# Eight lasting weight buffers from the output projection into the FFN, and a new order of the first FFN chunks

## The chip, the cores and the metric

The kernel runs on one core of one Trainium2 chip. The metric is the device time of one execution in microseconds (us), as the median of several runs. Engines are called PE (TensorE), ACT (ScalarE), DVE (VectorE), POOL (GpSimd) and SP (SyncE, which issues the DMAs here).

## The reference: what is computed

One decoder layer on 1024 tokens of width 1024, all in float32. Its second part is what the change touches:

```
mix = concat(o_mla, o_dil) @ w_o                 # (1024,1024) @ (1024,1024)
x   = x + g1 * mix
h2  = rms_norm(x) * (1 + scale2) + shift2
u   = causal depthwise conv3(h2 @ w_up)          # w_up (1024, 5632), columns [gate | value]
x   = x + g2 * ((silu(gate) * value) @ w_down)   # w_down (2816, 1024)
```

Ahead of it stand the adaptive norm, the input projection, a dense attention and a dilated attention, each with 8 heads. Their output lies in an SBUF buffer `mix` (features on the partitions, 8 blocks of 128 by 1024 tokens).

## The kernel before, in words

Each float32 matrix product is made of three products of rounded parts: an operand is split into a high part (ACT copies it into a rounding type) and a low part (original minus high part, on POOL for weights and on DVE for most activations), and PE computes high·high, high·low and low·high (`mm3`, L102 to L105).

The instructions are traced in program order. A planner then fixes the order on each engine: it takes, at each point of its own estimate of time, the instruction traced earliest among those that are ready and whose tile has a free buffer. The engines run their lists strictly in order. A tile with a tag shares that tag's buffers; a new tile waits until the old one in its buffer has been used for the last time. Pools that are closed give their memory to pools opened later, tile by tile. `tc.issue_after(ins)` orders what is traced in the block behind `ins` on the engine of `ins`.

**Output projection** (L783 to L817). Two halves `hf` of four row blocks (128 tokens each); per half four column chunks `cch` of 256. A chunk loads 1 MB of `w_o` as raw [128, 8, 256], multiplies it by the gate row `g1row` on DVE (L795), and splits it (`split_weights`, L85 to L100: one ACT copy of 2048 columns, four POOL subtractions of 512). There are two sets of raw, high and low buffers, one in the pool `wstream2`, one in `wmore2`; both are closed after the projection (L820, L821). PE runs, for each of the four row blocks, seven feature blocks (k = 0 to 6), then for each the eighth, which is kept apart (`last_pair`: `lhi`, `llo`, one buffer each). DVE adds the residual (L810), ACT squares it for the norm; after the last chunk of a half `normalized` (L743 to L757) computes the reciprocal root and writes the normalized rows back into `mix`. `h2_half(0)` (transposes on PE, evacuation with gain and shift, split) runs within the second half of the projection.

**FFN, up** (L823 to L1009). `w_up` is taken in 22 chunks of 256 columns (`todo`: gate and value columns in turn). A raw chunk is [128, 8, 256], tag `raw`, two buffers; split weight pieces are [128, 2, 4, 128], tag `wa`, eight buffers, all in the pool `fp`, opened after the projection's pools are closed. From the third chunk on (n = 2) a chunk is computed by Strassen's scheme on 2x2 blocks: seven products (`step`, in the order 1, 2, 6, 5, 7, 3, 4) of weight combinations (`up_parts`: three pieces straight from raw, four by sums on DVE, L849, tag `sum`, four buffers) and activation combinations TB[1] to TB[7]. Each product is 12 matmuls of 512 columns (`block_mm`, L877). Chunks 0 and 1 are computed directly: `direct_mm` of 24 matmuls per 128 columns and half, the first half (`h2[., 0]`) before the second half's transposes `h2_half(1)` in the trace, the rest in `direct_rest`. Meanwhile DVE makes the differences b11 to b21 in place in `mix` (L974); two of them go through DRAM (`t_s`) and come back in `sum` buffers (L988), to be split into the T tiles of a pool that takes `mix`'s place (L983 to L989). Then the weights of chunk 2 are loaded and split (`ahead`, L996); each later chunk's weights are made during the chunk before.

**FFN, down** (L1012 on) uses the same tags `raw` and `wa`.

Of the kernel before, what the change touches and what calls it, by code (L numbers as in the profile page):

```python
# [8 lines left out]
F32 = mybir.dt.float32  # L9
# [4 lines left out]
ALU = mybir.AluOpType  # L14
# [27 lines left out]
def hybrid_layer(ctx, tc, x, c, positions, w_ada, b_ada, g_mix_norm, w_in, g_q_lat, w_q_b, g_kv_lat, w_kv_b,  # L42
# [570 lines left out]

    psum_phase(x=3, o=2, s=3)
    phM = ExitStack()
    mxp = phM.enter_context(tc.tile_pool(name="mixbuf", bufs=1, reuse_waits="tile"))
    mix = mxp.tile([P, 8, S], F32, name="mix")
    wst2 = ExitStack()
    wpool[0] = wst2.enter_context(tc.tile_pool(name="wstream2", bufs=1, reuse_waits="tile"))
    ap = phB.enter_context(tc.tile_pool(name="phB", bufs=1, reuse_waits="tile"))  # L620
# [94 lines left out]

    phE = ExitStack()
    wst3 = ExitStack()
    more_weight_buffers(wst3.enter_context(tc.tile_pool(name="wmore2", bufs=1, side="right", reuse_waits="tile")), 1)

    def slot(shape, dt, name, tag="mA"):  # L720
        return sp.tile(shape, dt, tag=tag, name=name, bufs=4 if tag == "x1" else 8)

    ep = phE.enter_context(tc.tile_pool(name="phE", bufs=1, reuse_waits="tile"))
# [58 lines left out]

    mixTs = [mix_tiles(t) for t in range(NT)]  # L783
    for hf in range(2):
        mixT = mixTs[4 * hf:4 * hf + 4]
        lp_ = last_pair(hf)
        x1 = [slot([P, D], F32, "x1", "x1") for _ in range(4)]
        sse = [ep.tile([P, 4], F32, tag="ssE", name="ssE", bufs=8) for _ in range(4)]
        for cch in range(4):
            cs = slice(cch * 256, cch * 256 + 256)  # L790
            raw = raw_tile(KD, 256)
            with tc.issue_after(first_load):
                nc.sync.dma_start(raw[:, 0:4, :], w_o[512:1024, cs].rearrange("(k p) n -> p k n", p=P))
                nc.sync.dma_start(raw[:, 4:8, :], w_o[0:512, cs].rearrange("(k p) n -> p k n", p=P))
            V.tensor_tensor(raw, raw, g1row[:, None, cs].to_broadcast([P, KD, 256]), op=ALU.mult)  # L795
            w = split_weights(raw, KD, 256)
            pss = []
            for i in range(4):
                ps = bank()
                for k in range(E7):  # L800
                    mm3(ps[:, 0:256], (mixT[i][0][:, k, :], mixT[i][1][:, k, :]), (w[0][:, k, :], w[1][:, k, :]),
                        k == 0, False)
                pss.append(ps)
            for i in range(4):
# [4 lines left out]
                mm3(pss[i][:, 0:256], (lp_[0][:, ts_], lp_[1][:, ts_]), (w[0][:, E7, :], w[1][:, E7, :]), False, True)  # L809
                V.tensor_tensor(x1[i][:, cs], pss[i][:, 0:256], xr, op=ALU.add)  # L810
                junk = ep.tile([P, 256], BF16, tag="junk", name="junkE", bufs=1)
                A.activation(junk, x1[i][:, cs], AF.Square, accum_out=sse[i][:, cch:cch + 1])
                if cch == 3:
                    nc.sync.dma_start(x1_s[t], x1[i])
                    normalized(hf, i, sse[i], x1[i])
            if hf == 1 and cch < 3:
                h2_half(0, ((0, 1, 2), (3, 4, 5), (6, 7))[cch])  # L817

    phE.close()
    wst3.close()  # L820
    wst2.close()  # L821
    psum_phase(X=2, Y=2, Z=2, x=2)
# [3 lines left out]
    for _ in range(4):  # L826
        fp.tile([P, S], F32, tag="y", name="y", bufs=4)
    def parts(src, hi, lo, eng):
        A.activation(hi, src, AF.Copy)  # L829
        eng.tensor_tensor(lo, src, hi.bitcast(F32), op=ALU.subtract)  # L830

    def up_raw(ff2, which):
        c0 = which * FF + ff2 * 256
        raw = fp.tile([P, KD, 256], F32, tag="raw", name="raw", bufs=2)
        nc.sync.dma_start(raw, w_up[:, c0:c0 + 256].rearrange("(k p) n -> p k n", p=P))
        return raw

    def up_parts(raw, direct=False):
        a11, a21 = raw[:, 0:4, 0:P], raw[:, 0:4, P:256]
        a12, a22 = raw[:, 4:8, 0:P], raw[:, 4:8, P:256]  # L840

        def put(n, src):
            wt = fp.tile([P, 2, 4, P], F32R, tag="wa", name="wa", bufs=8)
            parts(src, wt[:, 0, :, :], wt[:, 1, :, :], G)
            w[n] = wt
# [6 lines left out]
        w = {}  # L852
        if direct:
            for n, src in (((0, 0), a11), ((0, 1), a12), ((1, 0), a21), ((1, 1), a22)):
                put(n, src)
            return w
        put(1, a11)
# [15 lines left out]
    def block_mm(ps, wt, blocks, first):  # L873
        for kt in range(4):
            hi, lo = blocks[kt]
            for m, (a, b) in enumerate(((0, hi), (0, lo), (1, hi))):
                T.matmul(four(ps), lhsT=wt[:, a, kt, :], rhs=b, start=(first and kt == 0 and m == 0),  # L877
                         stop=(kt == 3 and m == 2), skip_group_check=True)

# [3 lines left out]
    def direct_mm(ps, w, u, hf):  # L883
        for half in range(2):
            blocks = [(four(h2[4 * half + kt, hf][:, 0, :]), four(h2[4 * half + kt, hf][:, 1, :])) for kt in range(4)]
            block_mm(ps, w[u, half], blocks, half == 0)

# [55 lines left out]

    todo = [(ff2, which) for ff2 in range(NFF // 2) for which in range(2)]
    w01 = [up_parts(up_raw(*a), True) for a in todo[0:2]]
    ps01 = [[bank(tag) for tag in "XY"] for _ in range(2)]
    for u in range(2):
        direct_mm(ps01[0][u], w01[0], u, 0)
    h2_half(1, range(KD))
    for u in range(2):  # L950
# [20 lines left out]
    for kt in range(4):  # L971
# [40 lines left out]
    def down_parts(ff):  # L1012
        if ff % 2 == 0:
            down_parts.raw = fp.tile([P, 2, D], F32, tag="raw", name="raw", bufs=2)
            nc.sync.dma_start(down_parts.raw, w_down[ff * P:(ff + 2) * P, :].rearrange("(u p) n -> p u n", p=P))
        raw = down_parts.raw[:, ff % 2, :]
        hi, lo = [fp.tile([P, D], F32R, tag="wa", name="wd", bufs=8) for _ in range(2)]
# [89 lines left out]
```

## Time and profile before

| | us |
|---|---|
| median of 3 runs | 1450.82 (1448.73 to 1451.15) |
| profiled execution, own time | 1452.97 |
| its span | 1451.0 |

| engine | busy us | share |
|---|---|---|
| PE | 1376.4 | 95% |
| DVE | 972.6 | 67% |
| POOL | 795.5 | 55% |
| ACT | 727.4 | 50% |

How to read it: times in the trace run from the span's start. PE's matmuls are pipelined, so the durations of neighbours overlap; the rate is seen from start to start or from a row with many of them. "Idle before, releaser" is how long an engine stood still before a row and what ended it. The granted clock (PEclk) is a share of full speed: at 0.5 PE runs at 1.2 GHz, at 1.0 at 2.4 GHz. The attention ends at about 649 us, the projection's products run from 652 to 751.7 us, the up part of the FFN follows and ends shortly before 1206 us, and the down part runs to the end.

### The profile page before, as it was taken

How to read it: one execution, taken by the hardware profiler on the slowest of the kernel's cores; microseconds unless marked ns; L12 is line 12 of the kernel's file. 1: busy time of each engine (PE TensorE's matmuls, PEld its weight loads, DVE VectorE, ACT ScalarE, POOL GpSimd, SP SyncE). 2: the span in 40 equal slices, each digit the busy share in tenths (PEclk: the TensorE clock that was granted, in tenths of full speed). 3: DMA queues.
4: the chain of work that ended last, by engine and by line, in shares of the span. 5: the costliest groups of instructions: out<-in, count | busy, mean ns of one | idle time of the engine just before them, and what ended most of it. 6: DMA issues, size and time to landing. Idle time of an engine off the chain costs nothing.

```text
span 1451.0 us, 22006 instructions
## 1 busy us (share of the span) xinstructions
PE 1376.4 (95%) x7837; PEld 1178.1 (81%) x7837; DVE 972.6 (67%) x1834; ACT 727.4 (50%) x1409; POOL 795.5 (55%) x780
## 2 busy tenths in 40 slices
PE   5889999998999998989989799999999999999998
PEld 3789999996778786779978688888888887888887
DVE  3667888687878888875655767777777765226213
ACT  3524322376778887864444644455455454322320
POOL 3355656367766667534624275656655554555552
PEclk9999999999999999999999899999999999999999
DMA  9643354546121114003535122222222238445431
GB/s 320 197 149 120 125 184 158 112 152 212 31 59 45 59 45 116 2 17 124 195 114 177 59 97 76 88 88 71 75 87 88 87 113 307 162 144 191 160 113 58
DMA packets 140197, 173.31 MB, mean 119 GB/s; under 512 B 7986, under 2 KB 118968, under 8 KB 139960
## 3 DMA queue, kind: packets, MB, share of 16 engines
q1 hardware_dynamic: 140088, 171.92, 36.5%
q8 instruction: 61, 1.00, 0.3%
q14 instruction: 48, 0.39, 0.1%
HBM read 135.19 MB, written 36.70 MB: 118 GB/s over the span
## 4 chain that ended last, share of the span: by engine, by line
PE 63%; DVE 5%; DMA 4%; POOL 3%; ACT 3%; issue 3%; SPq 0%; DVEq 0%; POOLq 0%; ACTq 0%
PE d L1045 16%; PE X L877 16%; PE Z L877 8%; PE Y L877 5%; PE o L682 5%; PE s L639 4%; PE x L671 4%; DMA raw<-in_w_o_dram 2%; POOL w_lo L98 2%; PE p L103 1%; DVE pt L642 1%; PE p L104 1%; PE p L105 1%; ACT pt L646 1%; PE bank L105 1%
## 5 line engine op out<-in xcount | busy, mean ns | idle before, releaser
L1045 PE MATMUL d<-wd,m 128*128 128x512 f32 x1056 | 240.0, 389 | 3.2 <-ACT m L1028 3.0
L1045 PEld LDWEIGHTS d<-wd,m 128*128 128x128 f32 x1056 | 198.0, 188 | 45.1 <-ACT m L1028 3.4
L830 POOL TENSOR_TENSOR wa<-sum,wa 128x512 fp32r<-128x512 f32 x80 | 135.1, 1692 | 119.0 <-ACT wa L829 118.1
L1021 POOL TENSOR_TENSOR wd<-raw,wd 128x512 fp32r<-128x512 f32 x88 | 132.5, 1528 | 112.0 <-ACT wd L1018 96.3
L877 PE MATMUL X<-T,wa 128*128 128x512 f32 x720 | 172.2, 392 | 8.6 <-ACT wa L829 8.6
L103 PE MATMUL p<-w_hi,h_hi 128*128 128x256 f32 (+1 forms) x576 | 165.2, 288 | 3.2 <-ACT xn L362 3.2
L877 PEld LDWEIGHTS X<-T,wa 128*128 128x128 f32 x720 | 136.3, 190 | 37.6 <-ACT wa L829 9.0
L98 POOL TENSOR_TENSOR w_lo<-raw,w_hi 128x512 fp32r<-128x512 f32 (+3 forms) x74 | 109.8, 1514 | 97.8 <-ACT w_hi L92 97.8
L104 PE MATMUL p<-w_lo,h_hi 128*128 128x256 f32 (+1 forms) x576 | 163.4, 285 | 0.0
L105 PE MATMUL p<-w_hi,h_lo 128*128 128x256 f32 (+1 forms) x576 | 161.1, 286 | 1.0 <-DVE h_lo L262 1.0
L830 POOL TENSOR_TENSOR wa<-raw,wa 128x512 fp32r<-128x512 f32 x68 | 100.8, 1488 | 85.9 <-ACT wa L829 85.4
L1029 DVE TENSOR_TENSOR m<-m_raw,m 128x512 fp32r<-128x512 f32 x44 | 54.4, 1242 | 123.9 <-ACT m L1028 123.9
L1018 ACT ACTIVATE wd<-raw 128x1024 fp32r<-128x1024 f32 x44 | 46.6, 1059 | 142.6 <-PE d L1045 117.5
L647 POOL TENSOR_TENSOR st<-st,negone 128x1 f32<-128x1 f32 x128 | 69.9, 553 | 83.7 <-ACT pt L646 72.7
L103 PEld LDWEIGHTS p<-w_hi,h_hi 128*128 128x128 f32 x576 | 111.1, 193 | 3.6 <-ACT xn L362 3.4
L104 PEld LDWEIGHTS p<-w_lo,h_hi 128*128 128x128 f32 x576 | 111.4, 193 | 0.1
L678 DVE TENSOR_TENSOR pT_lo<-x,pT_hi 128x512 fp32r<-128x512 f32 (+1 forms) x160 | 98.0, 633 | 19.6 <-ACT pT_hi L677 18.5
L105 PEld LDWEIGHTS p<-w_hi,h_lo 128*128 128x128 f32 x576 | 109.0, 192 | 1.6 <-DVE h_lo L262 1.6
L677 ACT ACTIVATE pT_hi<-x 128x512 fp32r<-128x512 f32 (+1 forms) x160 | 86.0, 553 | 46.0 <-PE x L671 39.5
L929 DVE SCALAR_TENSOR_TENSOR y<-c,ccols,y 128x1023 f32<-128x1023 f32 x44 | 60.5, 1376 | 62.3 <-ACT y L928 61.5
L646 ACT ACTIVATE pt<-pt,st 128x256 f32<-128x256 f32 (+7 forms) x128 | 98.5, 772 | 6.3 <-DVE st L642 6.1
L648 POOL TENSOR_SCALAR pt<-pt,st 128x256 f32<-128x256 f32 (+7 forms) x128 | 97.6, 768 | 6.6
(265 smaller groups left out, 3385.4 us busy)
## 6 DMA issues: line engine op xcount, KB each, us to landing
raw<-in_w_up_dram SPq DMA_DIRECT2D x22, 1024.0 KB, 9.2
raw<-in_w_down_dram SPq DMA_DIRECT2D x22, 1024.0 KB, 5.1
raw<-in_w_ada_dram SPq DMA_DIRECT2D x16, 1024.0 KB, 8.2
m_s<-y SPq DMA_DIRECT2D x22, 512.0 KB, 2.6
m_raw<-m_s SPq DMA_DIRECT2D x44, 256.0 KB, 2.8
ada<-in_w_ada_dram SPq DMA_DIRECT2D x8, 1024.0 KB, 5.3
raw<-in_w_in_dram SPq DMA_DIRECT2D x8, 1024.0 KB
raw<-in_w_o_dram SPq DMA_DIRECT2D x16, 512.0 KB, 3.5
```

What stands on the lines that cost most here:

```text
L98: G.tensor_tensor(lo[:, i:i + 2, :], raw[:, i:i + 2, :], hi[:, i:i + 2, :].bitcast(F32), op=ALU.subtract)
L103: T.matmul(ps, lhsT=a[0], rhs=b[0], start=first, stop=False)
L104: T.matmul(ps, lhsT=a[0], rhs=b[1], start=False, stop=False)
L105: T.matmul(ps, lhsT=a[1], rhs=b[0], start=False, stop=last)
L646: A.activation(pt, pt, AF.Exp, bias=st[:, m:m + 1], scale=-1.0, accum_out=st[:, 2:3])
L648: G.tensor_scalar(pt, pt, st[:, 3:4], 1.0, op0=ALU.mult, op1=ALU.mult)
L677: A.activation(hi[:, 0:c0], px[:, 0:c0], AF.Copy)
L678: V.tensor_tensor(lo[:, 0:c0], px[:, 0:c0], hi[:, 0:c0].bitcast(F32), op=ALU.subtract)
L830: eng.tensor_tensor(lo, src, hi.bitcast(F32), op=ALU.subtract)
L877: T.matmul(four(ps), lhsT=wt[:, a, kt, :], rhs=b, start=(first and kt == 0 and m == 0), stop=(kt == 3 and m == 2), skip_group_check=True)
L1021: G.tensor_tensor(lo[:, cs], raw[:, cs], hi[:, cs].bitcast(F32), op=ALU.subtract)
L1045: T.matmul(pss[i, u], lhsT=m[a][:, ts_], rhs=w[b][:, cs], start=(ff == 0 and k == 0), stop=(ff == NFF - 1 and k == 2))
```

## The change

The projection and the FFN share eight weight buffers that stay to the end: four in a pool `wl` on the left side of SBUF, opened before `mix`, and four in `wr` on the right side, taken four and four in turns (`wa_tile`). Raw tiles have one buffer in each of `wl` and `wr`, and in the projection a third in `wthird`; `wstream2` and `wmore2` are gone. Projection weights are split in four pieces of two feature blocks. Except in the first chunk, a row block's eighth feature block follows its own seven. The first two FFN raw chunks are requested at the projection's end, before its pools are closed, and chunk 0 is split there; chunk 1 is split after. `h2_half(1)` is ordered behind the 24th matmul of `direct_mm`. The weights of chunk 2 are requested between `direct_rest(0)` and `direct_rest(1)` instead of behind the T loads. The `sum` buffers are opened with the other buffers of `fp`.

```
+    wl = ctx.enter_context(tc.tile_pool(name="wleft", bufs=1, reuse_waits="tile"))
     phM = ExitStack()
     ...
-    wst2 = ExitStack()
-    wpool[0] = wst2.enter_context(tc.tile_pool(name="wstream2", bufs=1, reuse_waits="tile"))
     ...
+    wr = ctx.enter_context(tc.tile_pool(name="wright", bufs=1, side="right", reuse_waits="tile"))
     wst3 = ExitStack()
-    more_weight_buffers(wst3.enter_context(tc.tile_pool(name="wmore2", bufs=1, side="right", reuse_waits="tile")), 1)
+    wt3 = wst3.enter_context(tc.tile_pool(name="wthird", bufs=1, side="right", reuse_waits="tile"))
+    n_wa, n_raw = [0], [0]
+    def wa_tile(shape):
+        pool = (wl, wr)[n_wa[0] // 4 % 2]
+        n_wa[0] += 1
+        return pool.tile(shape, F32R, tag="wa", name="wa", bufs=4)
+    def raw_stage(shape, pools_):
+        pool = pools_[n_raw[0] % len(pools_)]
+        n_raw[0] += 1
+        return pool.tile(shape, F32, tag="raw", name="raw", bufs=1)
+    def up_raw(ff2, which):
+        c0 = which * FF + ff2 * 256
+        raw = raw_stage([P, KD, 256], (wr, wl))
+        nc.sync.dma_start(raw, w_up[:, c0:c0 + 256].rearrange("(k p) n -> p k n", p=P))
+        return raw
     ...
+    def o_weights(cs):
+        raw = raw_stage([P, KD, 256], (wl, wt3, wr))
+        with tc.issue_after(first_load):
+            ...                                  # the two w_o loads as before
+        V.tensor_tensor(raw, raw, g1row[:, None, cs].to_broadcast([P, KD, 256]), op=ALU.mult)
+        w = []
+        for k in range(0, KD, 2):
+            wt = wa_tile([P, 2, 2, 256])
+            A.activation(wt[:, 0, :, :], raw[:, k:k + 2, :], AF.Copy)
+            G.tensor_tensor(wt[:, 1, :, :], raw[:, k:k + 2, :], wt[:, 0, :, :].bitcast(F32), op=ALU.subtract)
+            w += [(wt[:, 0, i, :], wt[:, 1, i, :]) for i in range(2)]
+        return w
     ...
-            w = split_weights(raw, KD, 256)
+            w = o_weights(cs)
+            def most(i):
+                pss[i] = bank()
+                for k in range(E7):
+                    mm3(pss[i][:, 0:256], (mixT[i][0][:, k, :], mixT[i][1][:, k, :]), w[k], k == 0, False)
+            if hf == 0 and cch == 0:
+                for i in range(4):
+                    most(i)
             for i in range(4):
+                if pss[i] is None:
+                    most(i)
     ...
+    n_raw[0] = 0
+    raws01 = [up_raw(0, i) for i in range(2)]
+    def direct_parts(raw):
+        w = {}
+        for u in range(2):
+            for half in range(2):
+                wt = wa_tile([P, 2, 4, P])
+                parts(raw[:, 4 * half:4 * half + 4, u * P:(u + 1) * P], wt[:, 0, :, :], wt[:, 1, :, :], G)
+                w[u, half] = wt
+        return w
+    w01 = [direct_parts(raws01[0])]
     phE.close()
     wst3.close()
-    wst2.close()
     ...
+        fp.tile([P, 4, P], F32, tag="s", name="sum", bufs=4)      # four times
     ...                                          # up_parts, down_parts: wa_tile and raw_stage in place of fp.tile
-    w01 = [up_parts(up_raw(*a), True) for a in todo[0:2]]
+    w01.append(direct_parts(raws01[1]))
     ps01 = [[bank(tag) for tag in "XY"] for _ in range(2)]
-    for u in range(2):
-        direct_mm(ps01[0][u], w01[0], u, 0)
-    h2_half(1, range(KD))
+    firsts = [direct_mm(ps01[0][u], w01[0], u, 0) for u in range(2)]
+    with tc.issue_after(firsts[0]):
+        h2_half(1, range(KD))
     ...
     direct_rest(0)
+    ahead = up_parts(up_raw(*todo[2]))
     direct_rest(1)
     ...
-            if n == 1:
-                ahead = up_parts(up_raw(*todo[2]))
```

`direct_mm` now returns its last matmul (`firsts[0]` is that of the first 128 columns).

## Rows read from the trace of the kernel before

**Rows 1.** The page, part 1: busy us, share of the span, instructions.
```profile
PE 1376.4 (95%) x7837; PEld 1178.1 (81%) x7837; DVE 972.6 (67%) x1834; ACT 727.4 (50%) x1409; POOL 795.5 (55%) x780
```

**Rows 2.** Windows: from:to, length, busy of PE, PEld, DVE, ACT, POOL; PEclk, DMA, GB/s.
```profile
656.00:751.60 95.60, 94.68 (x788) 93.90 (x786) 49.04 (x81) 37.56 (x83) 51.64 (x34) 1.00 0.37 123
751.60:768.30 16.70, 10.81 (x32) 7.01 (x32) 12.08 (x39) 11.85 (x27) 4.82 (x4) 0.59 0.72 252
768.30:816.20 47.90, 47.90 (x218) 39.57 (x216) 30.46 (x34) 26.04 (x39) 10.49 (x7) 1.00 0.40 121
816.20:830.00 13.80, 5.25 (x14) 3.89 (x13) 12.34 (x17) 6.50 (x12) 4.99 (x4) 0.63 0.33 114
830.00:1160.00 330.00, 329.72 (x1455) 272.65 (x1454) 251.08 (x207) 166.10 (x243) 202.48 (x126) 1.00 0.24 83
```

**Rows 3.** PE in order of time: start, us, operation, count [idle before, releaser].
```profile
751.38 0.28 PE L105 MATMUL bank<-w_hi,llo 128*128 128x256 f32 x1
754.61 0.53 PE L771 MATMUL x<-ident,mix 128*128 128x128 f32 x2 [2.96 <-DVE reye L748]
...
763.46 1.22 PE L877 MATMUL X<-h,wa 128*128 128x512 f32 x2 [0.19 <-ACT wa L829]
...
824.98 1.22 PE L877 MATMUL X<-T,wa 128*128 128x512 f32 x2 [8.55 <-ACT wa L829]
```

**Rows 4.** The chain that ended last, 600 to 1000 us: start, us, what.
```profile
739.72 0.44 PE x L771 x4
...
757.61 5.14 DMA raw<-in_w_up_dram
...
819.22 3.01 DMA sum<-t_s
...
823.61 0.61 DVE sum L849
824.30 0.56 ACT wa L829
...
863.52 5.44 PE X L877 x24
```

**Rows 5.** Waits of SP's queue, 640 to 840: us, times, longest.
```profile
SPq L835 <- DVE mix L757: 3.4, 1, 3.4
```

**Rows 6.** ACT in order of time, around 700 and 757 to 815.
```profile
700.44 0.63 ACT L739 ACTIVATE lhi<-mix 128x512 fp32r<-128x512 f32 x1
...
701.37 1.90 ACT L92 ACTIVATE w_hi<-raw 128x2048 fp32r<-128x2048 f32 x1
...
757.97 0.78 ACT L777 ACTIVATE mix<-x,modc,gm 128x512 f32<-128x512 f32 x1 [4.10 <-PE x L771]
758.65 0.77 ACT L779 ACTIVATE h<-x,modc,gm 128x512 fp32r<-128x512 f32 x1
...
762.77 2.19 ACT L829 ACTIVATE wa<-raw 128x512 fp32r<-128x512 f32 x4 [0.68 <-DMA raw<-in_w_up_dram]
...
814.24 2.18 ACT L829 ACTIVATE T<-sum 128x512 fp32r<-128x512 f32 x4
```

**Rows 7.** POOL in order of time: the first FFN pieces.
```profile
763.48 12.72 POOL L830 TENSOR_TENSOR wa<-raw,wa 128x512 fp32r<-128x512 f32 x8 [20.12 <-ACT wa L829]
```

**Rows 8.** SP in order of time: the first and the last T loads.
```profile
772.92 0.34 SPq L988 DMA_DIRECT2D sum<-t_s  x1
...
815.62 3.92 SPq L988 DMA_DIRECT2D sum<-t_s  x4
```

**Rows 9.** DVE in order of time, from 701 to 780.
```profile
701.10 0.69 DVE L740 TENSOR_TENSOR llo<-mix,lhi 128x512 fp32r<-128x512 f32 x1
...
715.36 2.29 DVE L795 TENSOR_TENSOR raw<-raw,g1row 128x2048 f32<-128x2048 f32 x1
...
768.17 1.78 DVE L974 TENSOR_TENSOR mix<-mix 128x512 f32<-128x512 f32 x1
...
779.87 0.69 DVE L974 TENSOR_TENSOR mix<-mix 128x512 f32<-128x512 f32 x1 [4.81 <-ACT mix L777]
```

More of the change, by code (lines that the diff above doesn't have):

```diff
@@ L783, in hybrid_layer @@
     mixTs = [mix_tiles(t) for t in range(NT)]
+    def o_weights(cs):
+        raw = raw_stage([P, KD, 256], (wl, wt3, wr))
+        with tc.issue_after(first_load):
+            nc.sync.dma_start(raw[:, 0:4, :], w_o[512:1024, cs].rearrange("(k p) n -> p k n", p=P))
+            nc.sync.dma_start(raw[:, 4:8, :], w_o[0:512, cs].rearrange("(k p) n -> p k n", p=P))
+        V.tensor_tensor(raw, raw, g1row[:, None, cs].to_broadcast([P, KD, 256]), op=ALU.mult)
[6 more added lines that the diff above has]
+        return w
     for hf in range(2):
@@ L790, in hybrid_layer @@
             cs = slice(cch * 256, cch * 256 + 256)
[L791 to L795, printed above, removed]
-            w = split_weights(raw, KD, 256)
-            pss = []
-            for i in range(4):
[L799 to L804, printed above, removed]
+            w = o_weights(cs)
+            pss = [None] * 4
+            def most(i):
[5 more added lines that the diff above has]
+                    most(i)
+            for i in range(4):
+                if pss[i] is None:
+                    most(i)
                 t = 4 * hf + i
@@ L808, in hybrid_layer @@
                 ts_ = slice(i * P, (i + 1) * P)
-                mm3(pss[i][:, 0:256], (lp_[0][:, ts_], lp_[1][:, ts_]), (w[0][:, E7, :], w[1][:, E7, :]), False, True)
+                mm3(pss[i][:, 0:256], (lp_[0][:, ts_], lp_[1][:, ts_]), w[E7], False, True)
                 V.tensor_tensor(x1[i][:, cs], pss[i][:, 0:256], xr, op=ALU.add)
@@ L817, in hybrid_layer, with parts @@
                 h2_half(0, ((0, 1, 2), (3, 4, 5), (6, 7))[cch])
+    n_raw[0] = 0
+    raws01 = [up_raw(0, i) for i in range(2)]
+    def parts(src, hi, lo, eng):
+        A.activation(hi, src, AF.Copy)
+        eng.tensor_tensor(lo, src, hi.bitcast(F32), op=ALU.subtract)
+    def direct_parts(raw):
[7 more added lines that the diff above has]
+    w01 = [direct_parts(raws01[0])]
     phE.close()
     wst3.close()
-    wst2.close()
     psum_phase(X=2, Y=2, Z=2, x=2)
@@ L827, in hybrid_layer, with up_parts @@
         fp.tile([P, S], F32, tag="y", name="y", bufs=4)
[L828 to L838, printed above, removed]
+        fp.tile([P, 4, P], F32, tag="s", name="sum", bufs=4)
+    def up_parts(raw):
         a11, a21 = raw[:, 0:4, 0:P], raw[:, 0:4, P:256]
@@ L842, in put @@
         def put(n, src):
-            wt = fp.tile([P, 2, 4, P], F32R, tag="wa", name="wa", bufs=8)
+            wt = wa_tile([P, 2, 4, P])
             parts(src, wt[:, 0, :, :], wt[:, 1, :, :], G)
@@ L852, in up_parts @@
         w = {}
[L853 to L856, printed above, removed]
         put(1, a11)
@@ L876, in block_mm @@
             for m, (a, b) in enumerate(((0, hi), (0, lo), (1, hi))):
-                T.matmul(four(ps), lhsT=wt[:, a, kt, :], rhs=b, start=(first and kt == 0 and m == 0),
-                         stop=(kt == 3 and m == 2), skip_group_check=True)
+                mm = T.matmul(four(ps), lhsT=wt[:, a, kt, :], rhs=b, start=(first and kt == 0 and m == 0),
+                              stop=(kt == 3 and m == 2), skip_group_check=True)
+        return mm.ins
     def product(ps, w, n, first=False):
@@ L885, in direct_mm @@
             blocks = [(four(h2[4 * half + kt, hf][:, 0, :]), four(h2[4 * half + kt, hf][:, 1, :])) for kt in range(4)]
-            block_mm(ps, w[u, half], blocks, half == 0)
+            ins = block_mm(ps, w[u, half], blocks, half == 0)
+        return ins
     class Chunk:
@@ L1013, in down_parts @@
         if ff % 2 == 0:
-            down_parts.raw = fp.tile([P, 2, D], F32, tag="raw", name="raw", bufs=2)
+            down_parts.raw = raw_stage([P, 2, D], (wr, wl))
             nc.sync.dma_start(down_parts.raw, w_down[ff * P:(ff + 2) * P, :].rearrange("(u p) n -> p u n", p=P))
         raw = down_parts.raw[:, ff % 2, :]
-        hi, lo = [fp.tile([P, D], F32R, tag="wa", name="wd", bufs=8) for _ in range(2)]
+        hi, lo = [wa_tile([P, D]) for _ in range(2)]
         A.activation(hi, raw, AF.Copy)
```

## The prediction

> **What bounds the kernel now.** I read the page's busy shares first: TensorE (PE) is busy 95% of the span and no other engine over 67% [rows 1]. A change away from PE pays only where PE stands still or runs at the lower clock, so next I cut the stretch that the diff touches into windows and looked at PE's busy time and granted clock in each [rows 2]. The projection (656.0 to 751.6 us) is full but for 0.92 us, at clock 1.00. Between 751.6 and 768.3 PE is busy 10.8 of 16.7 us at clock 0.59. The next 47.9 us are full. Between 816.2 and 830.0 it is busy 5.25 of 13.8 us at 0.63. From 830 to 1160 nothing is idle. So the diff meets two holes.
>
> **First hole.** PE's list shows the last projection product at 751.38, then transposes of the second half's normalized rows from 754.61, waiting for VectorE (DVE) or ScalarE (ACT), and the first FFN product only at 763.46 [rows 3]. Why no product earlier? In the chain of waits the FFN's raw weight load begins at 757.61 and takes 5.14 us [rows 4]; before it SP had waited 3.4 us for the last `normalized` write [rows 5], since the buffer lies on memory that the projection's end releases. ACT makes the high parts at 762.77 [rows 6], and GpSimd (POOL) had been idle for 20.12 us before its first low part [rows 7].
>
> **Second hole.** PE waits 8.55 us before 824.98 [rows 3]. The chain there reads backwards: ACT's weight part at 824.30, DVE's `sum` L849 at 823.61, DVE's T pieces, and a load `sum<-t_s` of 3.01 us [rows 4]. The `sum` tag has four buffers. The first T load takes one at 772.92, and the second four issue only at 815.62 [rows 8], because the first are split only after `mix` is given up (T on ACT from 814.24 [rows 6]). Chunk 2's Strassen sums are traced behind all eight loads and get a buffer last. It is a buffer order, not a shortage of engine time.
>
> **The change, part by part.** Full-rate prices: 24 products take 5.44 us, 0.227 us each; four transposes 0.44, 0.11 each [rows 4].
>
> (1) The first FFN chunk is loaded and split in the projection, into lasting buffers. Its raw uses the right pool's stage, free when projection chunk 5 is split; its four weight tiles take the left four, free when chunk 6's products end. At 788 instructions in 95.6 us [rows 2] one is 0.12 us, so a projection chunk's 96 last some 12 us, and chunk 6 ends near 739.5. Four ACT pieces take 2.19 us [rows 6] and four POOL pieces 12.72/8 = 1.59 us each [rows 7]: the last is ready at about 748. POOL's 20.12 us gap hides it; the margin is some 4 us, and without that cover up to the 11 us of load and split would stand on PE's path.
>
> (2) PE then has 48 products of chunk 0 on the first half (10.9 us, 751.7 to 762.6) with no new input. Chunk 1's four tiles follow projection chunk 7's, free at about 751.5; 0.55 us of ACT and 6.4 of POOL later they are there, near 759. Its 48 products, with the 32 transposes (3.5 us), carry PE to about 777.
>
> (3) The second half's transposes are ordered behind the first 24 products, so earliest at 757.1. Each feature needs two ACT evacuations, which start 0.68 us apart (757.97, next 758.65) [rows 6], so eight take 10.9 us. If they come behind all 48 products they end at 762.6 + 0.4 + 10.9 = 773.9, and one 0.69 us DVE low part later [rows 9] the last block is ready at 774.6, before the 777 at which the first is wanted. With two PSUM buffers PE may wait for an evacuation now and then: I take 0.5 us, bounds 0 and 2.3 (what the slow clock costs behind a hole: the 12 products from 824.98 to 830.0 take 5.0 us for a worth of 2.7).
>
> (4) What the first hole costs: in 751.6 to 768.3 stand 32 instructions [rows 2]: one projection product's end, 20 transposes, 11 FFN products. At full rate 20 x 0.11 + 11 x 0.227 = 4.7 us. 16.7 - 4.7 = **12.0 us** removed.
>
> (5) `up_parts` of chunk 2 moves ahead of the second direct product and of the T loads, so its four sums come first to the `sum` buffers, and its raw load (SP's queue, the stage that chunk 0 gave back before 751) is early. Sums, ACT pieces and POOL pieces for the first four tiles then fall under the 10.9 us of the second direct product; the other three wait for its buffers and are wanted 8 us and more later. In 816.2 to 830.0 stand 14 instructions [rows 2], two tails and 12 products, worth 2.7 us: 13.8 - 2.7 = **11.1 us** removed. What is late next: the T loads now wait for the sums. Products 1, 2, 6 and 5 cover 10.9 us and 7 and 3 another 5.4, against two rounds of four ACT pieces (2.18 us) [rows 6], DVE's pieces (0.69 each) [rows 9] and a 3 us load, some 11 us for both. Margin 5 us for the last product, less for product 7; I take a rest of 1.3 us, bounds 0 and 11.1 (the hole as it is).
>
> (6) The projection: four ACT pieces (2.19 us) in place of one of 1.90 [rows 6] per chunk, hidden by ACT's idle 58 of 95.6 us [rows 2]; three raw stages; and from the second chunk on the last product of a row block follows its own seven. Where the halves meet, it needs `lhi` and `llo`: `lhi` starts at 700.44 when the old half is done [rows 6], `llo` is there at 701.10 + 0.69 [rows 9], and PE would ask 21 products later, at 702.9. That leaves 1.1 us. Bounds -0.9 (the window's idle time) and +2.3, an L795 multiply of 2.29 us in front of `llo` [rows 9]. I take 0, the nearest row.
>
> Sum: 12.0 + 11.1 - 0.5 - 1.3 = 21.3 us. The profiled execution took 1452.97 us (span 1451.0), so 1431.7 for it; the median of the runs is 2.15 us lower, so 1450.82 - 21.3 = **1429.5 us**. After 830 PE is full, so nothing behind swallows it.
>
> **A rule weighed.** DVE's 128x512 subtraction takes 0.69 us alone and 1.78 us while POOL's pieces run [rows 7, 9]. The Trainium skill (SBUF — State Buffer, "Who interferes with whom") says that one of DVE's two SBUF port pairs is GpSimd's too, held as an exclusive lock by whoever comes first. The trace agrees in kind, 1.09 us more. By that rule chunk 2's earlier POOL pieces would lengthen the DVE steps beside them, which is rival C, 1434.6; without it, 1429.5.
>
> **Rivals.** (B) *The T loads keep the buffers.* If the planner lets them start before the sums, the second hole stays: 1450.82 - 12.0 + 0.5 = 1439.3. For: they took a buffer at 772.92 [rows 8]. Against: the sums are now traced first and their raw can be there before that. (C) *DVE becomes late.* POOL's seven pieces move to beside the 12 T pieces and four conv steps. If half of these 16 DVE steps take 1.09 us longer, that is 8.7 us, against the 17.4 us that DVE idles in 768.3 to 816.2 [rows 2] less the 11.5 by which the time before chunk 2 is squeezed; 2.8 us are left over, and 2.3 of slow clock behind the hole: 1434.6. For: the 1.78 us. Against: the same move takes chunk 0's pieces away from the L974 steps. (D) *First weights late*, the load standing behind blocked row loads on SP: the first hole stays, 1450.82 - 11.1 + 1.3 = 1441.0. Against: the stage is free a projection chunk or two before it is needed. (E) *Transposes end up behind both chunks' products*, at 773.5: PE waits about 8 us at 777, loses 2.3 to the clock, and what DVE makes of them starts 16 us later, so the second hole stays: 1450.82 - 1.7, about 1449. (F) *The other side: the split ring.* Eight buffers become two fours taken in turns. A piece waits for one named buffer, where any of eight would do, in each of the 20 FFN chunks that remain. If PE's interleaving of chunks frees them out of turn, a piece waits up to one product of 12 matmuls, 2.72 us. It decides only where POOL's reserve is gone: POOL is idle 127.5 of 330 us [rows 2], 7.4 of a chunk's 19.0 (84 x 0.227). With 1.5 us net per chunk: 1429.5 + 30 = 1459.5. Against: pieces are made in the order in which products use them.
>
> **Numbers.** Forecast 62%, B 14, C 9, D 5, E 4, F 6. The forecast alone spans 1425.5 (no rests, the projection's 0.9, and as much as the runs differ) to 1434; B, C and D reach to 1441. Range 1425.5 to 1441. About 0.2%, 2.9 us, can be told from no change: faster 0.90 (forecast, B, C, D), same 0.04 (E), slower 0.06 (F).
>
> **What would show it.** Right: no PE gap over 1 us between 751 and 830, clock 1.00 there; the first FFN `wa` parts near 740; chunk 2's first product near 799; `sum` L849 before its T loads. Wrong: a PE gap before product 6 or 7 of chunk 2 (B, C: the releaser tells which, a buffer held by a T load or a late DVE step), a wait for `wa` near 752 (D), transposes after 770 (E), gaps from `wa` in each FFN chunk (F).

## The result and the profile after

| | before | after |
|---|---|---|
| median, us (6 runs each, side by side) | 1450.21 (1447.21 to 1458.64) | 1435.43 (1432.25 to 1440.13) |
| ratio, 95% interval | | 0.9898 [0.9874, 0.9921] |
| profiled execution / its span | 1452.97 / 1451.0 | 1432.25 / 1430.5 |

The kernel became 14.8 us faster; 21.3 were forecast. Part 1 of the page after, as in [rows 1]: 8.9 us less PE time for the same 7837 matmuls, 10.6 us more DVE, 7.7 more POOL. Of the PE time 2.7 us are less ahead of the projection and 6.2 from there on, where part of the matmuls ran at the low clock before (0.59 and 0.63 in two windows of [rows 2]).

```profile
PE 1367.5 (96%) x7837; PEld 1172.4 (82%) x7837; DVE 983.2 (69%) x1834; ACT 726.4 (51%) x1433; POOL 803.2 (56%) x780
```

Windows of the kernel after, columns as in [rows 2]: the projection, the FFN up to the first T loads, chunks 1 to 3, and the rest of the up part.

```profile
652.00:750.40 98.40, 96.29 (x789) 95.91 (x789) 55.91 (x100) 46.87 (x118) 60.02 (x39) 0.98 0.50 161
750.40:793.80 43.40, 43.40 (x209) 36.02 (x208) 27.34 (x45) 20.98 (x36) 13.53 (x9) 1.00 0.32 102
793.80:842.00 48.20, 44.93 (x196) 36.15 (x195) 46.82 (x41) 32.88 (x51) 28.43 (x17) 1.00 0.34 109
842.00:1199.00 357.00, 354.95 (x1563) 292.67 (x1561) 271.93 (x221) 175.68 (x256) 212.25 (x131) 1.00 0.29 103
```

Both holes of [rows 2] are gone and the clock is 1.00 from 750 on. But PE still idles 2.1, 3.3 and 2.1 us in the first, third and fourth of these windows, and in the third DVE is busy 46.8 of 48.2 us. PE's list after, columns as in [rows 3]:

```profile
705.36 0.38 PE L105 MATMUL bank<-wa,llo 128*128 128x256 f32 x1 [2.11 <-DVE llo L757]
...
750.32 0.28 PE L105 MATMUL bank<-wa,llo 128*128 128x256 f32 x1
750.44 5.63 PE L911 MATMUL X<-h,wa 128*128 128x512 f32 x24
...
804.61 1.65 PE L911 MATMUL X<-h,wa 128*128 128x512 f32 x6 [0.81 <-POOL wa L854]
...
816.53 2.79 PE L911 MATMUL X<-T,wa 128*128 128x512 f32 x11 [1.21 <-ACT part L947]
...
834.84 0.73 PE L911 MATMUL Z<-T,wa 128*128 128x512 f32 x2 [1.25 <-ACT wa L853]
```

The first FFN product follows the last projection product after 0.12 us; in [rows 3] it came 12.1 us later. In place of the 8.55 us wait stand small ones with several releasers.

To add up the gain I cut both profiles at the first and last projection product, the first and last FFN product and the first down product:

| us | before | after | change | forecast |
|---|---|---|---|---|
| start to first projection product | 652.25 | 648.49 | -3.8 | 0 |
| projection | 99.12 | 101.82 | +2.7 | 0 |
| to the first FFN product | 12.08 | 0.12 | -12.0 | -11.5 |
| FFN, up | 439.67 | 434.98 | -4.7 | -9.8 |
| to the first down product | 3.37 | 0.23 | -3.1 | 0 |
| down, to the end | 244.50 | 244.83 | +0.3 | 0 |

From the projection on it is 16.8 us; the first line is work ahead of the change and, as the first experiment shows, scatter. The row of the first FFN product holds 20 transposes (2.2 us at full rate) that only move into the up part, and the up part before holds 2.3 us of slow clock behind the first hole; the two nearly cancel, so -12.0 is what the first hole gave. What PE lost inside the up part, each start-to-start step against the full rate of 0.227 us: 2.5 us in chunks 0 and 1, 11.7 in chunks 2 and 3 and nothing (-0.1) in 4 to 21 before; 0.3, 4.2 and 2.9 after.

### The profile page after: what moved, and what is told of

It is laid out like the page before. It is cut to its first block, busy times and chain, and to the rows that moved or that the text cites. A ratio compares the mean times of both kernels' runs of the same rounds, so it can differ in the third digit from the quotient of the medians.

```text
span 1430.5 us, 22067 instructions
## 1 busy us (share of the span) xinstructions
PE 1367.5 (96%) x7837; PEld 1172.4 (82%) x7837; DVE 983.2 (69%) x1834; ACT 726.4 (51%) x1433; POOL 803.2 (56%) x780
## 4 chain that ended last, share of the span: by engine, by line
PE 57%; DVE 7%; issue 6%; ACT 4%; POOL 4%; DMA 2%; SPq 0%; POOLq 0%; DVEq 0%; ACTq 0%
PE d L1080 16%; PE X L911 12%; PE Z L911 6%; PE o L681 5%; PE s L638 4%; PE x L670 4%; PE Y L911 3%; DMA raw<-in_w_o_dram 2%; POOL wa L811 1%; DVE sum L887 1%; POOL wa L854 1%; DVE y L965 1%; PE bank L105 1%; PE bank L103 1%; PE bank L104 1%
## 5 line engine op out<-in xcount | busy, mean ns | idle before, releaser
L1080 PE MATMUL d<-wa,m 128*128 128x512 f32 x1056 | 239.9, 389 | 0.6 <-DVE m L1064 0.6
L1080 PEld LDWEIGHTS d<-wa,m 128*128 128x128 f32 x1056 | 198.0, 188 | 42.3 <-DVE m L1064 1.2
L1056 POOL TENSOR_TENSOR wa<-raw,wa 128x512 fp32r<-128x512 f32 x88 | 133.8, 1542 | 104.6 <-ACT wa L1053 98.8
L854 POOL TENSOR_TENSOR wa<-raw,wa 128x512 fp32r<-128x512 f32 x68 | 104.7, 1545 | 107.7 <-ACT wa L853 102.2
L1053 ACT ACTIVATE wa<-raw 128x1024 fp32r<-128x1024 f32 x44 | 46.6, 1058 | 136.8 <-PE d L1080 120.9
L965 DVE SCALAR_TENSOR_TENSOR y<-c,ccols,y 128x1023 f32<-128x1023 f32 x44 | 69.0, 1571 | 44.0 <-ACT y L964 44.0
L120 POOL TENSOR_TENSOR rs_r<-rs_v,neghalf 128x4 f32<-128x4 f32 (+2 forms) x56 | 54.2, 971 | 71.7 <-DVE rs_v L119 64.2
```

What stands on the lines that cost most here:

```text
L965: V.scalar_tensor_tensor(y[:, 1:], in0=c[:, 0:S - 1], scalar=ccols[:, 88 + ch:89 + ch], in1=y[:, 1:], op0=ALU.mult, op1=ALU.add)
L1080: T.matmul(pss[i, u], lhsT=m[a][:, ts_], rhs=w[b][:, cs], start=(ff == 0 and k == 0), stop=(ff == NFF - 1 and k == 2))
```

## The experiments

All ratios are to the kernel before, with 95% intervals; "the stretch" is from the first projection product to the end (798.75 us before, 781.98 after). "Lost" is PE time against the full rate, as above.

**The changed kernel a second time**, with no edit.

> The changed kernel once more, nothing edited. Theory 1: the changed kernel gains 11.9 us in the first hole and 7.5 in the second, and loses 2.7 where the halves of the projection meet and 2.9 in stalls of later chunks; the 3.8 us by which attention ended sooner in its first profile and the 2.8 us at the start of the down part are differences between two executions, so this profile should show the same hole and stall places, attention ending within 645 to 650 us, and a ratio to before near 0.990. Rival: attention and the down part are really faster by the new order, then attention ends near 645.6 again and the down part starts with no gap again.

Measured: 1437.37 us, 0.9919 [0.9892, 0.9945]. In its profile the first projection product comes at 653.05 us instead of 648.49, and yet the stretch takes 781.96 instead of 781.98. So the executions differ in the attention part ahead. The down part starts after 0.23 us again, so that gain, against what I expected, is no scatter. In these profiles the change is worth 16.8 us where it acts, which lies within the interval of the first ratio (11.5 to 18.3 us) and above that of this one (8.0 to 15.7). But not every pair of profiles agrees so well: the projection takes 101.8 us in these two and 104.5 to 104.6 in three kernels below (chunk 2's sums behind, T loads without the sums' buffers, less DVE work) whose engines have the very same lists up to its end. So up to 2.8 us in the projection can turn on the execution, and single edits are compared below by the part in which they act.

**Chunk 2's sums behind again**: the one line goes back to where it was, the rest of the change stays.

```
     direct_rest(0)
-    ahead = up_parts(up_raw(*todo[2]))
     ...
+            if n == 1:
+                ahead = up_parts(up_raw(*todo[2]))
```

> Chunk 2's weights go back behind the T loads, all else as in the changed kernel. Theory 1 (the second hole is the order of the sum buffers): PE stops again before product 6 of chunk 2, for 6 to 9 us plus 2.3 of slow clock, and the time is 5 to 10 us above the changed kernel, about 1443. Rival (after the first hole is gone, DVE alone decides when chunk 2 runs, rival C): under 3 us, since DVE has the same steps to do.

Measured: 1445.78 us, 0.9971 [0.9958, 0.9985]; the stretch 794.33 us, lost in chunks 2 and 3: 16.5. PE's list, and DVE's around it:

```profile
820.26 1.22 PE L911 MATMUL X<-T,wa 128*128 128x512 f32 x2 [11.06 <-ACT wa L853]
```

```profile
816.52 1.29 DVE L854 TENSOR_TENSOR T<-sum,T 128x512 fp32r<-128x512 f32 x2
817.72 1.22 DVE L974 TENSOR_TENSOR y<-y 128x1024 f32<-128x1024 f32 x1
818.86 0.68 DVE L887 TENSOR_TENSOR sum<-sum,raw 128x512 f32<-128x512 f32 x1
819.46 0.68 DVE L887 TENSOR_TENSOR sum<-raw 128x512 f32<-128x512 f32 x1
```

The hole is back, at the same place and for the reason of [rows 4]: three of chunk 2's four sums come behind the last T pieces. That line closes the second hole. The stretch is 12.4 us longer, but 2.7 of that stand in the projection, which the edit does not reach (104.5 us); within the change the line is worth 10.4 us, in the up part (445.3 us against 435.0).

**The first FFN raw late**: both of the first raw loads wait for the last `x1` store. They go out at 752.6 us, 1.2 us behind the last projection product; in the kernel before it was 6.2 us behind.

```
-                    nc.sync.dma_start(x1_s[t], x1[i])
-    raws01 = [up_raw(0, i) for i in range(2)]
+                    last_store = nc.sync.dma_start(x1_s[t], x1[i]).ins
+    with tc.issue_after(last_store):
+        raws01 = [up_raw(0, i) for i in range(2)]
```

> The first two raw loads of the FFN are ordered behind the last store of the projection's rows on SP's queue, all else as in the changed kernel, buffers included. Theory 1 (the first hole was the late load): the load lands near 758, PE waits some 8 to 9 us with slow clock behind it, and the time is 9 to 12 us above the changed kernel, about 1446. Rival (the lasting weight tiles and the transposes' place made the gain, not the load): under 4 us.

Measured: 1446.89 us, 0.9976 [0.9958, 0.9995]; 10.8 us lost at the boundary, and in PE's list:

```profile
759.91 1.22 PE L912 MATMUL X<-h,wa 128*128 128x512 f32 x2 [8.22 <-ACT wa L854]
```

Without the early load nearly all of the first hole's gain is gone, though the lasting buffers and the place of the transposes stay: those two alone are worth little. Whether the load could be early without the lasting buffers was not tested.

**Transposes without their order**: the second half's transposes are free to go anywhere.

```
-    with tc.issue_after(firsts[0]):
-        h2_half(1, range(KD))
+    h2_half(1, range(KD))
```

> The order edge that puts the second half's transposes behind the first 24 products is left out; the planner then lists the first four transposes directly behind the projection, ahead of all products. Theory 1: PE waits at the projection's end for the last normalized row, which came at 756.0 against 750.4, so 5 to 6 us plus up to 2.3 us of slow clock: 5 to 8 us above the changed kernel, about 1442. Rival (the edge is of no account, since the other products are ready anyway): within 2 us.

Measured: 1437.14 us, 0.9922 [0.9892, 0.9951], the stretch 784.49, with 0.5 us from the last projection product to the first FFN product. My theory fell: with its weights there, the first product comes in time whether or not the transposes are told to wait. Without the order four transposes stand ahead of it (0.36 us at 755.22, before the last two row blocks were normalized), and the other 28 come behind 48 products all the same; what happens when all are put ahead is not shown. Of the 2.5 us by which the stretch is longer than the changed kernel's, 1.5 are the projection's.

**Two pairs of `lhi` and `llo`** against the stall at 705.36.

```
-        hi = ep.tile([P, 512], F32R, tag="lhi", name="lhi", bufs=1)
+        hi = ep.tile([P, 512], F32R, tag="lhi", name="lhi", bufs=2)      # llo likewise
```

> lhi and llo get two buffers each, all else as in the changed kernel, so the second half's pair can be split long before the halves meet. Theory 1: the 2.3 us wait for llo at the meeting of the halves goes, and nothing else changes: 2 to 2.5 us below the changed kernel from the projection's first product to the end (which took 781.97 us in two executions), so about 779.6. Rival: PE then waits there for something else that the same DVE multiply holds up (a row sum, a bank), and the stretch stays within 1 us of 782.

Measured: 1433.55 us, 0.9872 [0.9837, 0.9906], the stretch 782.11. The wait for `llo` goes, but the projection gains 0.4 us only (101.39 against 101.82). About 0.9 us are lost early, where PE waits for weight pieces of POOL (`wa` L811, at 667.1 and 668.4), and next in line behind the halves' meeting was

```profile
713.75 1.20 PE L788 MATMUL x<-ident,mix 128*128 128x128 f32 x9 [1.01 <-POOL mix L772]
```

**T loads without the sums' buffers**: they go straight into the place of their low part.

```
-            ts = fp.tile([P, 4, P], F32, tag="s", name="sum", bufs=4)
+            pair = tn.tile([P, 2, 512], F32R, name=f"T{n}{kt}")
+            ts = four(pair[:, 1, :]).bitcast(F32)
     ...                                          # the split writes to pair
```

> The eight T loads land in the low half of their own T tile and are split in place, so that they need no sum buffer; all else as in the changed kernel. Theory 2a (the stalls left in chunks 2 and 3, 4.2 us, come from T loads that wait for sum buffers, with ACT's list standing behind them): 2 to 4 us less there, 778 to 780 us from the projection's first product to the end. Rival 2b (DVE's list is full from 793 us on and is late whatever the buffers do): within 1 us of 782.

Measured: 1442.92 us, 0.9939 [0.9918, 0.9960]; lost 7.2 us in chunks 2 and 3 and 6.4 after. Worse: the up part is 6.6 us longer (the projection's 2.7 more are not the edit's). So it does not help to free the sums' buffers; the edit also gave the lists another order, and what that cost is not told apart.

**The sums' move alone**, on the kernel before: its eight common buffers and its first hole stay.

```
     direct_rest(0)
+    ahead = up_parts(up_raw(*todo[2]))
     direct_rest(1)
     ...
-            if n == 1:
-                ahead = up_parts(up_raw(*todo[2]))
```

> The kernel before, with chunk 2's weights moved between the two direct remainders and nothing else. Theory 1: the second hole goes (11.7 us lost there before, 0 to 4 after), the first stays at 12 us: ratio to before about 0.994 (8 to 10 us). The lost 3.1 us at the start of the down part, which the changed kernel does not show, tells whether that gain belongs to this part (then it goes here too) or to the buffers (then it stays). Rival (the hole is only filled once the first hole is gone): within 3 us of before.

Measured: 1451.94 us, 1.0005 [0.9978, 1.0032]: nothing. The down part starts 3.15 us late as before, so that gain is not the sums' move's. The second hole does go (lost in chunks 2 and 3: 3.0 us in place of 11.7), but 9.1 us are lost in chunks 4 to 21, where the kernel before lost none. PE's list has the same wait every 39 us, in six places from 876.6 to 1072.0:

```profile
915.69 1.65 PE L877 MATMUL X<-T,wa 128*128 128x512 f32 x6 [0.75 <-DVE c L918]
...
954.76 1.43 PE L877 MATMUL X<-T,wa 128*128 128x512 f32 x5 [0.75 <-DVE c L918]
...
993.84 1.43 PE L877 MATMUL X<-T,wa 128*128 128x512 f32 x5 [0.75 <-DVE c L918]
```

DVE's list and POOL's ahead of the second of these:

```profile
946.59 1.27 DVE L931 SCALAR_TENSOR_TENSOR y<-c,ccols,y 128x1022 f32<-128x1022 f32 x1
947.78 1.77 DVE L849 TENSOR_TENSOR sum<-sum,raw 128x512 f32<-128x512 f32 x1
949.48 1.21 DVE L938 TENSOR_TENSOR y<-y 128x1024 f32<-128x1024 f32 x1
950.61 1.77 DVE L849 TENSOR_TENSOR sum<-raw 128x512 f32<-128x512 f32 x1
952.31 1.80 DVE L849 TENSOR_TENSOR sum<-raw,sum 128x512 f32<-128x512 f32 x1
954.03 0.68 DVE L918 TENSOR_TENSOR c<-X,part 128x512 f32<-128x512 f32 x1
```

```profile
946.66 2.34 POOL L830 TENSOR_TENSOR wa<-sum,wa 128x512 fp32r<-128x512 f32 x1 [0.55 <-ACT wa L829]
949.55 2.28 POOL L830 TENSOR_TENSOR wa<-raw,wa 128x512 fp32r<-128x512 f32 x1 [0.55 <-ACT wa L829]
952.27 1.29 POOL L830 TENSOR_TENSOR wa<-raw,wa 128x512 fp32r<-128x512 f32 x1 [0.43 <-ACT wa L829]
```

They take turns. POOL's piece at 946.66 starts 0.07 us behind a DVE step and takes 1.05 us longer than the 1.29 of the last one; DVE's sum at 947.78 starts while that piece runs, and takes 1.77 where it takes 0.68 alone; the piece at 949.55 starts behind the gate's multiply and takes 2.28. So each of the three sums is lengthened by 1.1 us, and `c` L918, which PE needs, comes behind them. `c` itself, with one input in PSUM, keeps 0.68. This is what the Trainium skill says (SBUF — State Buffer, "Who interferes with whom"): a DVE instruction with two SBUF inputs and a POOL instruction that reads SBUF exclude each other, and whoever comes second waits.

**The T pieces' low parts on POOL** (the last four), on the changed kernel.

```
-            ... split_block(ts, tn.tile([P, 2, 512], F32R, name=f"T{n}{kt}"), V)
+            ... split_block(ts, tn.tile([P, 2, 512], F32R, name=f"T{n}{kt}"), G if v else V)
```

> The low parts of the last four T tiles are made on POOL in place of DVE, all else as in the changed kernel: 2.7 us less for DVE, some 5.2 more for POOL, which stood idle for 12 us there. Rival 2b (DVE late) expects 2 to 4 us less in chunks 2 and 3, 778 to 780 from the projection's first product to the end. Theory 2a (buffers and ACT's list) expects within 1 us of 782.

Measured: 1440.02 us, 0.9915 [0.9885, 0.9946], lost 6.2 and 4.2 us where the changed kernel lost 4.2 and 2.9. Neither expectation came: work that leaves DVE for POOL did not help.

**Less DVE work in chunks 2 to 21**, once on the changed kernel, once on the kernel with the sums' move alone. The kernels then leave out part of the convolution. The theory by now: DVE is late, by steps that lengthen beside POOL's.

```
-        V.scalar_tensor_tensor(y[:, 2:], in0=c[:, 0:S - 2], ...)
+        if last:                       # False for chunks 2 to 21
+            V.scalar_tensor_tensor(y[:, 2:], in0=c[:, 0:S - 2], ...)
```

> The changed kernel, with the second conv step left out in FFN chunks 2 to 21 (so that part of the computation is missing): VectorE has two steps of 1.96 us less in each chunk of 19 us. In the changed kernel PE loses 4.2 us in chunks 2 and 3 and 2.9 us in chunks 4 to 21. Theory L (VectorE is the late one: its steps lengthen beside GpSimd's pieces and its adds come late): both losses fall, together from 7.1 to under 3 us, and the stretch from the first projection product to the end falls from 782.0 to about 777 us. Rival M (the order in which each engine's list is laid out holds PE, not VectorE's load): the loss stays within 2 us of 7.1 or merely moves between chunks.

> The kernel before with chunk 2's sums moved alone, which lost 9.1 us in chunks 4 to 21, some 0.9 us every 39 us; here the second conv step is left out in chunks 2 to 21 (so that part of the computation is missing). Theory L (a late VectorE add, c L918, from steps that lengthen beside GpSimd's pieces): the 9.1 us fall below 2, and the time goes to about 1444 us, 0.995 of the kernel before. Rival M (the order of the lists): at least 6 of the 9.1 us stay, and the ratio stays within 0.998 to 1.003.

Measured, changed kernel: 1431.40 us, 0.9870 [0.9847, 0.9893]; lost 2.0 and 1.4 us in place of 4.2 and 2.9. That is 3.4 together: half goes, a little less than expected, and the projection lost 2.7 more in this profile (9.0 against 6.3), so the stretch is only 1.7 shorter. Gone are the wait at 834.84 and both waits for DVE's `c` (0.94 us before 863.64 and 1.07 before 902.85); the waits in chunk 2 stay (one is shorter, but comes before anything that the edit reaches), and a wait of 1.13 us comes in chunk 21. Sums' move alone: 1438.59 us, 0.9921 [0.9896, 0.9946], better than expected; in chunks 4 to 21 it lost nothing (-0.1) in place of 9.1. The windows 840 to 1180 of three kernels, columns as in [rows 2]. Before:

```profile
840.00:1180.00 340.00, 340.00 (x1501) 281.53 (x1500) 261.23 (x215) 173.56 (x254) 203.02 (x128) 1.00 0.24 82
```

The sums' move alone:

```profile
840.00:1180.00 340.00, 332.63 (x1453) 271.31 (x1452) 275.73 (x210) 166.70 (x249) 221.57 (x125) 1.00 0.25 82
```

The same with the conv step left out:

```profile
840.00:1180.00 340.00, 340.00 (x1500) 281.50 (x1501) 194.09 (x176) 169.51 (x253) 181.28 (x127) 1.00 0.24 84
```

Read POOL's column: 125 pieces take 221.6 us, and 127 take 181.3 once 36 DVE steps are gone, though nothing of POOL's was touched. Between the first two windows the work is the same, or a little less, and DVE and POOL are both longer, by 14.5 and 18.6 us. For the sums' move alone the lateness is shown: it is DVE's and POOL's time in each other's way, and the order in which their lists happen to meet decides how much. For the changed kernel it is shown for the half that goes.

**Split ring alone**: the kernel before, with its eight buffers as two tags of four in turns.

```
-            wt = fp.tile([P, 2, 4, P], F32R, tag="wa", name="wa", bufs=8)
+            wt = turn([P, 2, 4, P], F32R, "wa", 4, 4)   # tags wa0, wa1, bufs=4, four and four; raw0, raw1 likewise
```

> The kernel before, with one edit: the FFN's and the down stage's eight weight buffers become two tags of four taken in turns, and the two raw stages two tags of one. Nothing else of the change is in it; both holes stay. My theory: pieces are made in the order in which products use them, so the 20 FFN chunks keep their 439.7 us within 1.5 us; and if the ring is what starts the down stage 3.1 us earlier in the changed kernel, the 3.4 us there fall to 0.3 and the ratio is 0.998. Rival: the 3.1 us come from the order of the lists and stay; ratio 1.000. Rival F of the prediction: each chunk waits for a named buffer, 1.5 us a chunk, 30 us in all, ratio 1.02.

Measured: 1449.60 us, 0.9997 [0.9977, 1.0017]. The up part takes 440.81 us against 439.67, so the prediction's rival F (1.5 us a chunk) is out. The down part starts 1.08 us after the last FFN product, not 3.37. Before, then with the split ring:

```profile
1206.50 1.67 PE L1045 MATMUL d<-wd,m 128*128 128x512 f32 x6 [2.98 <-ACT m L1028]
```

```profile
1203.58 2.79 PE L1052 MATMUL d<-wa,m 128*128 128x512 f32 x11 [0.69 <-ACT c L931]
```

So 2.3 us (3.37 - 1.08) of the 3.1 that the changed kernel gains there come with the ring; in the lists the first `m` part stands ahead of the last conv step and no longer behind it. Where the other 0.8 comes from is open.

**The gate's multiply on POOL**, on the kernel with two pairs.

```
-            V.tensor_tensor(yg[u], yg[u], yv[u], op=ALU.mult)
+            (G if ff2 else V).tensor_tensor(yg[u], yg[u], yv[u], op=ALU.mult)
```

> The kernel with two pairs of lhi and llo, and the gate's multiply moved from VectorE to GpSimd from the second pair of FFN chunks on: VectorE has one step of 1.78 us less per chunk, GpSimd one more, estimated at 2.6 us from two pieces of 1.29, of the 7.3 us that it idles in a chunk of 19. Theory L: VectorE's adds come earlier, of the 7.0 us lost in chunks 2 to 21 about 3 go, and the time is about 1431 us. Rival (GpSimd becomes the late one): weight pieces queue behind the multiply, PE waits for wa in chunks 4 to 21, and the time is 1437 us or more.

Measured: 1450.88 us, 1.0013 [0.9990, 1.0036]; lost in chunks 4 to 21: 20.6 us. Slower, as the rival had it, but not by its wait. PE's groups of lines from 840 to 1180, and POOL's:

```profile
L911 PE MATMUL X<-T,wa 128*128 128x512 f32 x612 | 148.1, 394 | 10.2 <-DVE c L954 7.4 <-ACT part L938 2.8
...
L911 PE MATMUL X<-h,wa 128*128 128x512 f32 x199 | 49.4, 391 | 4.7 <-ACT c L960 4.7
```

```profile
L974 POOL TENSOR_TENSOR y<-y 128x1024 f32<-128x1024 f32 x18 | 46.5, 2583 | 34.4 <-PE Z L911 10.4 <-DVE y L967 8.1 <-PE X L911 5.8
```

PE waits for DVE and ACT there, never for `wa`. One step further back, though, POOL is the late one. At PE's longest wait POOL's, DVE's and PE's lists show:

```profile
896.81 2.78 POOL L974 TENSOR_TENSOR y<-y 128x1024 f32<-128x1024 f32 x1 [1.16 <-DVE y L967]
```

```profile
900.85 1.73 DVE L887 TENSOR_TENSOR sum<-raw 128x512 f32<-128x512 f32 x1 [3.52 <-POOL wa L854]
```

```profile
903.24 2.33 PE L911 MATMUL X<-T,wa 128*128 128x512 f32 x5 [3.29 <-DVE c L954]
```

The multiply stands in front of POOL's weight pieces, DVE's next sum waits for a `sum` buffer that such a piece still reads, and `c` comes behind that sum. From 840 to 1180 DVE's sums wait 36.1 us in this way, against 26.1 in the changed kernel and 16.6 in the kernel before. So the rival was right about who is late, and the loss reaches PE by the `sum` buffers.

How much DVE and POOL have to do in turns can be estimated from undisturbed durations of these traces. A chunk has four sums of 0.68, four conv steps of 1.27, one multiply of 1.21 and seven POOL pieces of 1.29: 18.0 us of DVE and POOL together in a chunk of 19.0. Without the second conv step it is 15.5. This sum is a warning and not a price: with 18.0 the kernel before loses nothing in chunks 4 to 21 and the sums' move alone 9.1 us. It also counts too much: from 820.25 to 842 the changed kernel gets 24.7 us of such work done in 21.8 (11.8 POOL pieces, 6.5 sums, four conv steps), in part because neighbours on one engine overlap (sums of 0.68 us start 0.60 apart at 818.86). How much of an instruction shuts the other engine out is not shown.

## Why the prediction was right or wrong

The sign, the mechanism of both holes and the range were right; the measured 1435.4 us lies outside the forecast's own 1425.5 to 1434, near rival C's 1434.6. That nearness is partly luck: the 2.7 us lost in the projection and the 3.1 us found at the down part, which stand in neither sum, nearly cancel. Of its own signs, chunk 2's first product (797.74, 799 named) and the early sums came, but so did a gap over 1 us in chunk 2. By its steps, from one pair of profiles:

- **Steps 1 to 4, the first hole: right.** Forecast 11.5 us net, measured 12.0. The first pieces are there well ahead, as POOL's list shows (four from 737.00; the forecast was 740, ready by 748):

```profile
737.00 5.50 POOL L854 TENSOR_TENSOR wa<-raw,wa 128x512 fp32r<-128x512 f32 x4 [4.84 <-ACT wa L853]
```

  The load's place did it (10.8 us come back when it is late); telling the transposes to wait, to which step 3 gave a calculation of its own, is of no account, since without it most of them stand behind the products too.

- **Step 5, the second hole: right mechanism, the rest mis-sized.** The sums come 35 us ahead of the first T load, DVE's row and SP's:

```profile
755.99 0.68 DVE L887 TENSOR_TENSOR sum<-raw 128x512 f32<-128x512 f32 x1
```

```profile
791.37 0.33 SPq L1025 DMA_DIRECT2D sum<-t_s  x1
```

  The rest was taken as 1.3 us; chunks 2 and 3 lose 4.2. PE's three waits there have three causes: at 804.61 a piece of POOL's, at 816.53 an ACT copy behind T pieces whose loads came late, at 834.84 an ACT piece behind a late conv step of DVE. ACT's rows ahead of the last two:

```profile
813.03 1.34 ACT L853 ACTIVATE T<-sum 128x512 fp32r<-128x512 f32 x2 [2.98 <-DMA sum<-t_s]
...
833.21 1.06 ACT L973 ACTIVATE y<-y 128x1024 f32<-128x1024 f32 x1 [4.98 <-DVE y L967]
```

  The margin of 5 us counted ACT's pieces, DVE's T pieces and a load, each at its undisturbed duration and with no other work between them, and left out that the conv steps, the sums and POOL's pieces of the same 48 us stand in each other's way: DVE is busy 97% of that window. That is rival C, given 9%: of DVE's 17.4 idle us there it left 5.9, for 8.7 us of longer steps, and held against it that chunk 0's pieces leave the L974 steps. It is shown for the third wait, which goes with the conv step. For the first two it is argued only, and the second turns on the T loads as well.

- **"After 830 PE is full, so nothing behind swallows it": wrong, 2.9 us.** That PE is busy 329.72 of 330 us [rows 2] says that PE was the last to be ready, not how close the others were. By the estimate above 18.0 of a chunk's 19.0 us were taken on DVE and POOL together, and as PE lost nothing, a new order of their lists could only cost. Both waits for `c` in the changed kernel go when DVE has less to do. With the sums' move alone this swallowed the whole gain (9.1 us lost for 8.7 won).

- **Step 6, the projection: 0 taken, +2.7 measured, above the upper bound of 2.3.** That bound names the right cause, a gate-row multiply in front of `llo`, and it was longer than in [rows 9] (3.33 against 2.29 us). DVE's list:

```profile
700.30 3.33 DVE L806 TENSOR_TENSOR raw<-raw,g1row 128x2048 f32<-128x2048 f32 x1 [0.75 <-POOL mix L772]
...
704.01 1.29 DVE L757 TENSOR_TENSOR llo<-mix,lhi 128x512 fp32r<-128x512 f32 x1
```

  PE asked at 703.1 and got `llo` at 705.3. The margin of 1.1 us was read from a list whose order the change was free to alter. Against the kernel before this wait costs 2.6 us. The other two parts nearly cancel: 1.6 us less is lost behind it, where the kernel before had waits of its own, and 1.6 more in the first 7 us, where the clock stays at its low level (0.5) for 6.8 us in place of 3.4, granted 0.53 in the mean against 0.76. Whether that is the change's doing is open: the mean was 0.51 in the kernel with the sums' move alone, whose lists up to there are those of before, and 0.76 in the kernel with chunk 2's sums behind, whose lists are the changed kernel's.

- **Not foreseen: the down part starts 3.1 us earlier.** The hole of 3.37 us before the first down product is in no step, since the windows stopped at 1160. 2.3 us of it go with the ring, to which the prediction gave only costs.

The sum by the stages: 21.3 forecast, less 5.1 in the up part and 2.7 in the projection, 0.5 more in the first hole, 3.1 found, 0.3 lost in the down part: 16.8 us.

Rivals: B, D, E and F did not come; the sums went first, the weights were early, the transposes stood between the products, and the ring alone made the up part 1.1 us longer. C came in part: chunks 2 and 3 lost 2.9 us more than the forecast's rest, of the 5.1 it priced, without its slow clock (1.00) and with the T loads for one of the causes, and it went on beyond them.

## What to carry to other kernels

Where PE is full, add up the undisturbed durations of the engines that exclude each other, per round of the loop, before calling the stretch safe: at 18.0 of 19.0 us (an estimate) one order of the lists cost nothing and another 9.1 us, with no work added. A wait removed ahead of such a stretch is to be tested alone, too; here the sums' move was worth nothing by itself and 10.4 us with the rest. And look at every hole in the span, not only at those that the diff names: 3 us came from one that no one had counted.

## What the runs showed of the hardware that was not expected

DVE's two-input steps and POOL's pieces lengthen each other in both directions, by about the time that is left of the other's instruction (0.68 to 1.77 us, and 1.29 to 2.34), while DVE adds with one input in PSUM keep 0.68 us throughout. And of one and the same program two executions differ by 4.6 us ahead of the projection and by 0.02 us in the 782 us behind it, while the projection, with the same lists on every engine, took 101.8 to 104.6 us over the kernels of this case.
